# Turning the modulation's partial sums into columns: four products with a 0/1 matrix, or four transposes and a sum on VectorE

## The chip, the cores and the metric

One core of one Trainium2 chip runs the whole program in one launch. The metric is the device time of one execution in microseconds (us); a lower time is better. The engines are TensorE (PE, with its weight loads as PEld), VectorE (DVE), ScalarE (ACT), GpSimd (POOL) and SyncE (SP), which here only issues transfers.

## The reference, cut to what matters

Two blocks follow each other on a sequence of 256 tokens by 1024 channels, with a context of the same size. Both begin with a modulation: a condition vector and a context condition vector go through a large matrix, and the result, cut into pieces of 1024, scales, shifts and gates the tokens.

```
cond, cond_ctx = silu(c), silu(c_ctx)
mod   = cond     @ w_mod + b_mod      # 1024 -> 6*1024 (first block), 3*1024 twice (second)
mod_c = cond_ctx @ w_mod + b_mod
h  = rms_norm(x,   g) * (1 + sc1) + sh1
hc = rms_norm(ctx, g) * (1 + csc1) + csh1
y  = token_mixer(h, hc, ...)          # first block; then peer_ffn over 16384 experts
...                                   # second block: attention, pooling, neighbourhood attention
```

Everything is float32.

## The kernel before, in words

**The modulation.** The wide matrices are streamed in pieces of 128 x 1024. `mod_gen` computes 512 columns of one modulation: four pieces `mraw` arrive by SP's queue (L196), and eight matmuls per 512 columns (L211) write into one PSUM tile `modps`. The contraction of 1024 is cut into eight slices of 128; slice k goes to the row group 32*(k % 4), so that rows 32g and 32g+1 of `modps` hold the partial sum of group g for the two conditions, and the other rows are zero. VectorE copies `modps` to `modP` (L216). What is wanted is a column layout: channel on the partition, condition on the free axis. `mod_cols` makes it: for each of the four blocks of 128 columns a product with the 128 x 2 matrix `sel2`, which has ones at rows 32g+j of column j, adds the four groups and turns rows to columns at once (L231). VectorE adds the bias and writes the columns (L232). This runs 24 times: 4 times ahead of the first projection (`front`, tile `m`), 8 times beside the first block's mixers (`later`, tiles `m2`, `g1c`, `g2c`), 12 times beside the expert stage (`mods2`, tiles `mc` and `gc`).

**What runs around it.** Every large projection streams its weights: a piece `raw` arrives, ScalarE rounds it to `wH` (L78), VectorE subtracts to get `wL` (L79), and three matmuls (L116, L117, L118) use them. In the expert stage each of 128 tiles `ups` takes one such piece and 24 matmuls, while VectorE also does a top-k search. Then one-hot products (`pmps`, L992, `farps`, L977) pick activations, and 64 batches of four indirect loads `vrow` (L1035, issued by POOL) with eight matmuls `vacc` each (L1041) sum the chosen rows. The second half of these batches runs beside the second block's context half (`ch`, `ccat`). The rows fill 9 or 13 buffers, and a buffer comes free when its matmuls have run.

**What sets the order.** The engines execute in program order, each its own. The framework that builds the program sorts the instructions of each engine by times that it estimates itself; only those marked `keep_in_program_order` keep the written order. A change at 24 places therefore moves instructions elsewhere.

Of the kernel before, what the change touches and what calls it, by code (L numbers as in the profile page):

```python
# [15 lines left out]
ALU = mybir.AluOpType  # L16
AX = mybir.AxisListType
# [3 lines left out]
P = 128  # L21
# [23 lines left out]
class Builder:  # L45
# [178 lines left out]
    def mod_cols(self, dst, m, bias):  # L224


        nc = self.nc
        n = dst.shape[2]
        ps = self.ps((P, 4, 2), name="mcps")
        for b in range(4):  # L230
            nc.tensor.matmul(ps[:, b], m[:, b * P:(b + 1) * P], self.sel2, start=True, stop=True)  # L231
        nc.vector.tensor_tensor(dst, ps[:, :, 0:n], bias[:, :, None].to_broadcast([P, 4, n]), op=ALU.add)  # L232

    def row(self, dst, cols):

# [80 lines left out]
    def consts(self):  # L316
        cp, nc = self.cp, self.nc
        self.ident = self.load(cp, [P, P], "ident")
        self.sel2 = self.load(cp, [P, 2], "sel2")
        self.one = cp.tile([P, 1], F32, name="one")  # L320
        nc.gpsimd.memset(self.one, 1.0)
        self.bcol = self.load(cp, [P, 48], "b_cols")
        self.bcol2 = self.load(cp, [P, 2, 24], "b_cols_2")
        self.ms = cp.tile([P, 2, 2], F32, name="ms")
        self.half = cp.tile([P, 16], F32, name="half")
        nc.gpsimd.memset(self.half, -0.5)
        self.bp, self.Kc = None, []
        self.mcols = [cp.tile([P, 2, 8, 2], F32, name=f"mc{l}") for l in range(2)]
# [1240 lines left out]
def lay(i):  # L1569
    f = np.float32  # L1570
    r = {}
    tok = lambda a: np.ascontiguousarray(a.reshape(2, P, D).transpose(1, 0, 2))
    r["ident"] = np.eye(P, dtype=f)
    s2 = np.zeros((P, 2), f)
    for g in range(4):
        for j in range(2):
            s2[32 * g + j, j] = 1
    r["sel2"] = s2
    r["x"], r["ctx"] = tok(i["x"]), tok(i["ctx"])
    two = lambda a, b: np.ascontiguousarray(np.stack([a.reshape(D), b.reshape(D)], -1).reshape(8, P, 2).transpose(1, 0, 2))  # L1580
    r["cond"] = two(i["c"], i["c_ctx"])
# [7 lines left out]
    for d in range(2):  # L1589
        for typ in range(2):  # L1590
            dst = 32 * d + (64 if typ == 0 else 0)
# [90 lines left out]
```

## Time and profile before

| | |
|---|---|
| time, median of 3 runs | 1552.82 us (1551.61 to 1557.32) |
| the profiled execution | 1545.91 us, its span 1544.0 us |
| PE busy | 1436.1 us, 93% of the span |
| DVE busy | 924.0 us, 60% |
| ACT busy | 693.7 us, 45% |
| POOL busy | 383.1 us, 25% |
| mean granted clock of TensorE | 0.965 |

The span is the time from the first to the last instruction in the profiled execution; 1.9 us of its own time lie around it. A busy PE means that a matmul is in flight; matmuls overlap, so the distance between two starts tells more than the duration of one.

### The profile page before, as it was taken

To read this page: it belongs to the slowest core of one execution; us is meant where nothing else is said; L and a number is where in the kernel's file an instruction comes from. 1 tells how busy PE (TensorE), PEld (TensorE's weight loads), DVE (VectorE), ACT (ScalarE), POOL (GpSimd) and SP (SyncE) were. 2 spreads that over 40 slices of the span, in tenths; PEclk is the share of its full clock that TensorE was granted. 3 is DMA by queue.
4 is the path that set the end of the run, shared out by engine and by line. 5 is a ranking of instruction groups with operands and counts; after the bars stand their busy time and mean duration, and the time that the engine had idled before them with its cause. 6 is when DMAs were issued, how large, how long until landed. Compare 5 with 4: busy or idle time off the path is not lost.

```text
span 1544.0 us, 26118 instructions
## 1 busy us (share of the span) xinstructions
PE 1436.1 (93%) x10090; PEld 1122.3 (73%) x10090; DVE 924.0 (60%) x2284; ACT 693.7 (45%) x1152; POOL 383.1 (25%) x380
## 2 busy tenths in 40 slices
PE   7999997899999999999999998687979779998998
PEld 3677764798888899999977776334635458866976
DVE  4478464679998444444355554544334478867875
ACT  4354242444444455555444444332333355645653
POOL 1100001000000000000356664565567714012201
PEclk9999997999999999999989999798989999999999
DMA  9535344356886865666779997889998936414521
GB/s 358 167 132 171 108 133 150 125 172 213 306 290 241 304 187 186 190 189 186 238 306 349 357 353 289 305 308 341 344 334 280 349 121 209 153 55 155 182 80 41
DMA packets 97180, 345.80 MB, mean 224 GB/s; under 512 B 12705, under 2 KB 14241, under 8 KB 95777
## 3 DMA queue, kind: packets, MB, share of 16 engines
q1 hardware_dynamic: 54576, 198.73, 37.9%
q0 software_dynamic: 36864, 134.23, 23.7%
q10 hardware_dynamic: 5616, 11.18, 2.4%
q8 instruction: 79, 1.29, 0.3%
q14 instruction: 45, 0.36, 0.1%
HBM read 343.05 MB, written 1.05 MB: 223 GB/s over the span
## 4 chain that ended last, share of the span: by engine, by line
PE 86%; DMA 4%; DVE 4%; POOL 2%; issue 2%; ACT 2%; ACTq 0%; POOLq 0%; DVEq 0%
PE acc L116 10%; PE acc L118 10%; PE acc L117 9%; PE ups L116 8%; PE ups L118 8%; PE ups L117 8%; PE pmps L992 7%; PE vacc L1041 7%; PE modps L211 4%; DMA vrow<-in_v_dram,at 2%; PE tps L1491 2%; PE pvo L1497 2%; POOL vrow L1035 1%; PE mcps L231 1%; PE farps L977 1%
## 5 line engine op out<-in xcount | busy, mean ns | idle before, releaser
L79 DVE TENSOR_TENSOR wL<-raw,wH 128x1024 fp32r<-128x1024 f32 x269 | 337.1, 1253 | 245.9 <-ACT wH L78 244.5
L78 ACT CAST wH<-raw 128x1024 fp32r<-128x1024 f32 x277 | 290.3, 1050 | 369.2 <-PE ups L117 148.8
L1035 POOL DMA_INDIRECT vrow<-in_v_dram,at x256 | 252.8, 987 | 615.1 <-DVE wL L79 440.1
L116 PE MATMUL ups<-h2T,wH 128*128 128x256 f32 x1024 | 287.7, 281 | 0.0
L118 PE MATMUL ups<-h2T,wL 128*128 128x256 f32 x1024 | 286.5, 281 | 0.0
L117 PE MATMUL ups<-h2T,wH 128*128 128x256 f32 x1024 | 285.7, 279 | 0.0
L116 PEld LDWEIGHTS ups<-h2T,wH 128*128 128x128 f32 x1024 | 192.5, 188 | 14.3 <-issue 5.0
L118 PEld LDWEIGHTS ups<-h2T,wL 128*128 128x128 f32 x1024 | 192.1, 188 | 8.4 <-DVE tkc L826 1.7
L117 PEld LDWEIGHTS ups<-h2T,wH 128*128 128x128 f32 x1024 | 192.5, 188 | 0.0
L1041 PE MATMUL vacc<-vrow,Z 128*32 128x512 f32 x1024 | 147.4, 647 | 26.8 <-DMA vrow<-in_v_dram,at 26.8
L995 DVE SCALAR_TENSOR_TENSOR junk<-iota,sel,pmps 128x128 f32<-128x128 f32 x256 | 89.0, 348 | 96.2 <-PE pmps L992 89.5
L992 PE MATMUL pmps<-ATa,oh 128*128 128x72 f32 x512 | 104.8, 287 | 1.8 <-ACT oh L981 1.8
L992 PE MATMUL pmps<-ATb,oh 128*128 128x56 f32 x512 | 98.1, 274 | 0.0
L1041 PEld LDWEIGHTS vacc<-vrow,Z 128*32 128x32 f32 x1024 | 29.5, 114 | 89.6 <-issue 55.0
L980 ACT ACTIVATE oh<-farps,place 128x512 f32<-128x512 f32 x64 | 43.9, 687 | 87.0 <-PE farps L977 87.0
L992 PEld LDWEIGHTS pmps<-ATa,oh 128*128 128x128 f32 x512 | 80.2, 197 | 2.0 <-ACT oh L981 2.0
L992 PEld LDWEIGHTS pmps<-ATb,oh 128*128 128x128 f32 x512 | 80.3, 198 | 1.7 <-issue 1.7
L211 PE MATMUL modps<-mraw,condP 128*32 128x512 f32 x192 | 43.5, 677 | 16.5 <-DVE condP L186 8.3
L1480 ACT ACTIVATE smp<-sps,smst 128x512 f32<-128x512 f32 (+1 forms) x72 | 44.5, 619 | 28.9 <-DVE smst L1478 25.7
L921 ACT COPY ATa<-ups 128x256 f32<-128x256 f32 x72 | 47.5, 660 | 21.7 <-PE ups L118 21.7
L1478 DVE TENSOR_REDUCE smst<-sps 128x1 f32<-128x512 f32 (+1 forms) x72 | 42.5, 597 | 18.8 <-PE sps L1474 18.2
L116 PE MATMUL acc<-wL,xh 128*128 128x512 f32 (+1 forms) x128 | 48.4, 378 | 3.4 <-DVE wL L79 3.4
(407 smaller groups left out, 2926.2 us busy)
## 6 DMA issues: line engine op xcount, KB each, us to landing
raw<-in_u_dram SPq DMA_DIRECT2D x128, 512.0 KB, 3.8
mraw<-in_w_mod_dram SPq DMA_DIRECT2D x96, 512.0 KB, 4.5
raw<-in_w_in_dram SPq DMA_DIRECT2D x40, 512.0 KB, 4.9
raw<-in_w_out_dram SPq DMA_DIRECT2D x32, 512.0 KB, 3.6
raw<-in_w_gate_dram SPq DMA_DIRECT2D x24, 512.0 KB, 4.1
raw<-in_peer_wq_dram SPq DMA_DIRECT2D x16, 512.0 KB, 3.6
vrow<-in_v_dram,at POOLq DMA_INDIRECT x256, 6.3
raw<-in_w_nv_dram SPq DMA_DIRECT2D x8, 512.0 KB, 5.4
```

Of the source, the lines that this page charges most:

```text
L78: self.pin(nc.scalar.copy(H, raw))
L79: self.pin((low or nc.vector).tensor_sub(L, raw, H.bitcast(F32)))
L116: mm(ps, a[0], b[1], start=start, stop=False)
L117: mm(ps, a[0], b[0], start=False, stop=False)
L118: mm(ps, a[1], b[0], start=False, stop=stop)
L211: nc.tensor.matmul(ps[g:g + 32], cond[:, k], raw[k // 2][:, k % 2 * 512:(k % 2 + 1) * 512], start=k < 4, stop=k >= 4, tile_position=(0, g))
L921: nc.scalar.copy(acts[0][:, :, i1] if i1 < R0 else acts[1][:, :, i1 - R0], ps)
L992: nc.tensor.matmul(pm[:, i, r0:r1], oh[:, i], a[:, tb * P + t], start=True, stop=True)
L995: nc.vector.scalar_tensor_tensor(junk, self.iota, sel[:, 0, c:c + 1], pm[:, i], op0=ALU.is_equal, op1=ALU.mult, accum_out=act[:, c:c + 1])
L1035: nc.gpsimd.indirect_dma_start(v, None, rows, bass.IndirectOffsetOnAxis(ap=at[:, c:c + 1], axis=0))
L1041: tc.keep_in_program_order(nc.tensor.matmul(out[2 * tb + dh][32 * g:32 * g + 32], Z[:, b - b0, g], V[g][:, dh * 512:(dh + 1) * 512], start ...
L1480: nc.scalar.activation(p, ps, AF.Exp, bias=st[:, 0:1], accum_out=st[:, 1:2])
```

## The change

`mod_cols` transposes each 128 x 128 block of `modP` (by a matmul with the identity) into a PSUM tile of four times 128 columns. There the four partial sums of a condition lie 32 columns apart. VectorE sums over the four (a reduction that reads 4 x n x 4 elements per partition, n being 1 or 2, and writes 4 x n), and then adds the bias in place. The matrix `sel2` and its load fall away.

```
-        ps = self.ps((P, 4, 2), name="mcps")
+        ps = self.ps((P, 4, 4, 32), name="mcps")
         for b in range(4):
-            nc.tensor.matmul(ps[:, b], m[:, b * P:(b + 1) * P], self.sel2, start=True, stop=True)
-        nc.vector.tensor_tensor(dst, ps[:, :, 0:n], bias[:, :, None].to_broadcast([P, 4, n]), op=ALU.add)
+            nc.tensor.transpose(ps[:, b].rearrange("p g r -> p (g r)"), m[:, b * P:(b + 1) * P], self.ident)
+        nc.vector.reduce_sum(dst, ps[:, :, :, 0:n].rearrange("p b g r -> p b r g"), axis=AX.X)
+        nc.vector.tensor_tensor(dst, dst, bias[:, :, None].to_broadcast([P, 4, n]), op=ALU.add)
...
     def consts(self):
         cp, nc = self.cp, self.nc
         self.ident = self.load(cp, [P, P], "ident")
-        self.sel2 = self.load(cp, [P, 2], "sel2")
```

Lines behind `mod_cols` move by one up to `consts` (L288 becomes L289), and are the same behind it.

The order of the instructions changes at many places. Three matter here.

On PE, in the expert stage, the rows around one of the twelve calls (the 20th of 24), before:

```order
L116 MATMUL ups<-h2T_2390,wH 128x256
L117 MATMUL ups<-h2T_2388,wH 128x256
L231 MATMUL mcps<-sel_91,modP 128x2 x4
L118 MATMUL ups<-h2T_2388,wL 128x256
L116 MATMUL ups<-h2T_2391,wH 128x256
```

and of the change:

```order
L116 MATMUL ups<-h2T_2400,wH 128x256
L117 MATMUL ups<-h2T_2398,wH 128x256
L231 MATMUL mcps<-ident,modP 128x128 x4
L118 MATMUL ups<-h2T_2398,wL 128x256
L116 MATMUL ups<-h2T_2401,wH 128x256
```

Here nothing moved; four products have become four transposes at the same place.

On VectorE, at the end of `front`, where the second half of the channels gets its scale `a` and the affine step (`nhf`, `hT`) starts, before:

```order
L232 TENSOR_TENSOR m_75<-mcps,b_cols 128x8
L432 SCALAR_TENSOR_TENSOR a_77<-m_75,norm_g 128x8
L79 TENSOR_TENSOR wL<-raw,wH 128x1024
L288 TENSOR_SCALAR nhf<-xT,a_77,m_75 128x256 x3
L289 TENSOR_TENSOR hT_74<-nhf,hT_73 128x256 x2
```

and of the change:

```order
L79 TENSOR_TENSOR wL<-raw,wH 128x1024
L232 TENSOR_REDUCE m_75<-mcps 128x8
L233 TENSOR_TENSOR m_75<-m_75,b_cols 128x8
L432 SCALAR_TENSOR_TENSOR a_77<-m_75,norm_g 128x8
L289 TENSOR_SCALAR nhf<-xT,a_77,m_75 128x256 x3
L290 TENSOR_TENSOR hT_74<-nhf,hT_73 128x256 x2
```

The subtraction `wL` that stood between the scale and the affine step stands ahead of both now.

On PE, at the end of the expert rows, from the context's second norm (`nps<-ident,ctx`) on, with projections of the context left out at the dots, before:

```order
L1041 MATMUL vacc<-vrow,Z 32x512 x8
L278 MATMUL nps<-ident,ctx_9813 128x128 x16
L1041 MATMUL vacc<-vrow,Z 32x512 x8
...
L1041 MATMUL vacc<-vrow,Z 32x512 x2
...
L1041 MATMUL vacc<-vrow,Z 32x512 x14
L1321 MATMUL fps<-ident,kk 128x128 x12
```

and of the change:

```order
L1041 MATMUL vacc<-vrow,Z 32x512 x8
L279 MATMUL nps<-ident,ctx_9835 128x128 x16
L1041 MATMUL vacc<-vrow,Z 32x512 x8
...
L1041 MATMUL vacc<-vrow,Z 32x512 x8
...
L1041 MATMUL vacc<-vrow,Z 32x512 x10
L1321 MATMUL fps<-ident,kk 128x128 x2
L1041 MATMUL vacc<-vrow,Z 32x512 x6
L1321 MATMUL fps<-ident,kk 128x128 x6
L1041 MATMUL vacc<-vrow,Z 32x512 x8
```

Behind that norm stand 24 matmuls `vacc` (three batches) before, and 40 (five batches) now: two batches have moved behind it.

## Rows read from the trace of the kernel before

**Rows 1.** The page: busy time by engine, and the chain by engine

```profile
PE 1436.1 (93%) x10090; PEld 1122.3 (73%) x10090; DVE 924.0 (60%) x2284; ACT 693.7 (45%) x1152; POOL 383.1 (25%) x380
PE 86%; DMA 4%; DVE 4%; POOL 2%; issue 2%; ACT 2%; ACTq 0%; POOLq 0%; DVEq 0%
```

**Rows 2.** Windows: length, busy time of PE, PEld, DVE, ACT, POOL, clock, DMA

```profile
71.00:200.00 129.00, 129.00 (x777) 93.46 (x774) 83.68 (x154) 54.35 (x93) 5.10 (x5) 1.00 0.42 139
366.00:480.00 114.00, 114.00 (x899) 95.64 (x898) 109.68 (x388) 50.63 (x63) 0.00 (x0) 1.00 0.77 281
480.00:560.00 80.00, 80.00 (x662) 70.30 (x661) 44.91 (x56) 36.56 (x45) 0.00 (x0) 1.00 0.71 256
```

**Rows 3.** The view of the tile mcps: count, duration min/median/max in ns, first and last start

```profile
L231 PE MATMUL mcps<-sel,modP x192: 165/251/272, 16.9 to 552.1; 128*128 128x2 f32 x192
L232 DVE TENSOR_TENSOR mc<-mcps,b_cols x8: 141/156/166, 393.6 to 496.5; 128x8 f32<-128x8 f32 x8
```

**Rows 4.** Timeline of PE in the expert stage: start, length, instruction

```profile
429.70 0.95 PE L231 MATMUL mcps<-sel,modP 128*128 128x2 f32 x8
430.51 0.36 PE L116 MATMUL ups<-h2T,wH 128*128 128x256 f32 x1
```

**Rows 5.** Timeline of PE at four transposes in the mixers

```profile
133.18 0.60 PE L644 MATMUL kstp<-ident,de 128*128 128x128 f32 x4
133.53 0.37 PE L116 MATMUL acc<-hT,wH 128*128 128x256 f32 x1
```

**Rows 6.** Timeline of PE at the last two modulations of the mixers

```profile
256.46 1.05 PE L231 MATMUL mcps<-sel,modP 128*128 128x2 f32 x8 [1.22 <-DVE modP L216]
259.85 3.20 PE L211 MATMUL modps<-mraw,condP 128*32 128x512 f32 x8 [2.33 <-DMA mraw<-in_w_mod_dram]
269.97 1.05 PE L231 MATMUL mcps<-sel,modP 128*128 128x2 f32 x8 [0.80 <-DVE modP L216]
270.89 1.96 PE L241 MATMUL mrps<-modR,one 128*128 128x512 f32 x4
```

**Rows 7.** Timeline at the end of front, brackets: idle before and its releaser

```profile
45.29 0.95 PE L231 MATMUL mcps<-sel,modP 128*128 128x2 f32 x8
46.28 0.17 DVE L232 TENSOR_TENSOR m<-mcps,b_cols 128x8 f32<-128x8 f32 x1 [1.35 <-PE mcps L231]
46.56 1.22 DVE L79 TENSOR_TENSOR wL<-raw,wH 128x1024 fp32r<-128x1024 f32 x1
47.70 1.05 DVE L288 TENSOR_SCALAR nhf<-xT,a,m 128x256 f32<-128x256 f32 x3
49.14 0.39 PE L116 MATMUL acc<-hT,wH 128*128 128x256 f32 x1 [2.90 <-DVE hT L289]
```

**Rows 8.** Groups by line and shape, DVE: count, busy us, mean ns, idle before

```profile
L1478 DVE TENSOR_REDUCE smst<-sps 128x1 f32<-128x512 f32 x48 | 32.8, 687 | 7.2 <-PE sps L1474 6.8
L1478 DVE TENSOR_REDUCE smst<-sps 128x1 f32<-128x256 f32 x24 | 9.7, 417 | 11.6 <-PE sps L1474 11.4
L1268 DVE TENSOR_REDUCE hss<-raw 128x2 f32<-128x128 f32 x8 | 2.3, 284 | 3.4 <-ACT raw L1267 3.4
```

**Rows 9.** Timeline: a wL, and the first matmul that reads it

```profile
400.07 1.20 DVE L79 TENSOR_TENSOR wL<-raw,wH 128x1024 fp32r<-128x1024 f32 x1
403.07 0.28 PE L118 MATMUL ups<-h2T,wL 128*128 128x256 f32 x1
```

**Rows 10.** The view of line L644: the transposes of the tile kstp

```profile
L644 PE MATMUL kstp<-ident,de x16: 270/273/328, 97.9 to 145.3; 128*128 128x128 f32 x16
```

**Rows 11.** Waits of PE from 956 to 1244: us in total, times, longest

```profile
PE vacc L1041 <- DMA vrow<-in_v_dram,at: 26.8, 9, 5.7
```

**Rows 12.** Windows of the tile vacc: length, PE, PEld, DVE, clock, DMA share, GB/s

```profile
956.00:1244.00 288.00, 84.20 (x520) 16.04 (x520) 1.36 (x2) 0.91 0.88 319
```

**Rows 13.** Timeline: the first one-hot products, with the idle time before

```profile
764.88 0.44 PE L992 MATMUL pmps<-ATa,oh 128*128 128x72 f32 x2 [1.81 <-ACT oh L981]
```

**Rows 14.** Windows of all engines at the start of the one-hot products

```profile
767.00:781.00 14.00, 14.00 (x73) 10.89 (x71) 4.91 (x27) 5.45 (x8) 2.77 (x4) 0.51 0.56 226
```

More of the change, by code (lines that the diff above doesn't have):

```diff
@@ L1573, in lay @@
     r["ident"] = np.eye(P, dtype=f)
[L1574 to L1578, printed above, removed]
     r["x"], r["ctx"] = tok(i["x"]), tok(i["ctx"])
```

## The prediction

> **What bounds the kernel now.** I read the page first: PE is busy for 93% of the span, and the chain that ended last runs over PE for 86% of it [rows 1]. So time that PE saves should count, if it is saved where PE itself is the limit. Shares of a span don't tell that, so the windows by stage come next. From 71 to 200 us and from 366 to 560 us PE is busy for the whole window at a granted clock of 1.00 [rows 2]; the reader should look at DVE in the same rows: 109.68 of 114 us from 366 to 480, so there a second engine is nearly full. The view of the tile mcps says where the change sits: 192 matmul records for 24 calls, so eight records for four products, between 16.9 and 552.1 us [rows 3]. Of the 24 calls four lie ahead of 50 us, four from 71 to 200 us, four from 205 to 271 us, and twelve from 366 to 560 us.
>
> **What the products cost and what the transposes will.** A duration of 251 ns each [rows 3] is no price, because matmuls overlap. The price on PE is the distance from the first of a group to the next other instruction: 429.70 to 430.51, which is 0.81 us for eight records [rows 4]. Four transposes of 128 x 128 already stand in this kernel, each with one record: 133.18 to 133.53, which is 0.35 us [rows 5]. They write to PSUM and read float32 as the new ones do, so I take that price: a call saves 0.81 - 0.35 = 0.46 us of PE.
>
> - Expert stage, 12 calls: PE never pauses there, and the place of the call among its neighbours is unchanged (the first order extract). 12 x 0.46 = 5.5 us.
> - Mixers from 71 to 200 us, 4 calls, PE full too: 1.8 us.
> - 205 to 271 us, 4 calls. Behind the third PE waits 2.33 us for a transfer anyway [rows 6], so nothing is gained there. At the last, the row product follows in program order at 270.89, 0.92 us after the start at 269.97 [rows 6]; PE waits for modP ahead of it, so the saving shows at once. I count three calls at 0.4: 1.2 us.
> - Front, 4 calls. At the last one the reader can follow a latency: product at 45.29, columns at 46.28, a subtraction wL from 46.56, the affine step from 47.70, and PE, idle for 2.90 us, goes on at 49.14 [rows 7]. The transposes take 0.46 off that. The new order also puts wL ahead of the scale (the second extract), which would take up to 1.2 us more off, if the modulation's own pieces don't arrive later than that. The same swap stands at the first half of the channels. Bounds: 0 (transfers set the end) and 3 us (both swaps and the latency in full). I take 1.5 us, the middle, since PE works between these points and only part of what is moved away from the path comes back.
>
> Sum of what is saved: 5.5 + 1.8 + 1.2 + 1.5 = 10.0 us.
>
> **What is added.** A reduction on VectorE that reads 32 elements per partition (16 where n is 1) from PSUM, strided. The trace has no such size, but 512 elements took 687 ns, 256 took 417, and 128 (from SBUF) 284 [rows 8]; the slope is 270/256 = 1.05 ns per element, so 32 elements give 417 - 224 x 1.05 = 0.18 us. Bounds: 0.15 us, as short as an addition over 8 columns (156 ns [rows 3]), and 0.28 us, as the reduction over 128. I take 0.18. The addition of the bias stays, from SBUF; as long as now. So 24 x 0.18 = 4.3 us on VectorE. Where does it lie? In the expert stage behind the lead of wL: the wL that begins at 400.07 ends at 401.27, and the first matmul that reads it starts at 403.07, 1.80 us later [rows 9]. That is the shortest lead that I found from 366 to 480 us; the other tiles there have more. The seven calls there bring 7 x (0.46 + 0.18) = 4.5 us of drift against VectorE's 4.3 us of idle time in that window (114 - 109.68 [rows 2]), so the cover is just enough in the mean. If it weren't, PE would wait for wL. On the path the reduction stands only where PE waits for the columns, in front and at the last calls of the mixers: about six calls, 6 x 0.18 = 1.1 us. The load of sel2 (128 x 2) falls away; it lies beside the first pieces of x, and I count nothing: PE waits for those.
>
> Net: 10.0 - 1.1 = 8.9 us. Against the profiled execution 1545.91 - 8.9 = 1537.0 us. That execution was 6.9 us below the median of the runs (1552.82), so the same difference taken from the median gives 1552.82 - 8.9 = **1543.9 us**, 0.57% less. About 0.5% (7.8 us) is what a measurement of this kernel can tell from no change.
>
> [...] In the row, four transposes hold PE for 0.35 us, and PE's clock stays at 1.00 from 71 to 200 us with the 16 transposes of kstp inside it [rows 2, 5, 10]. [...]
>
> **The rivals.**
>
> *The new order helps further.* PE waits 26.8 us in nine waits for expert rows between 956 and 1244 us [rows 11]. With vacc moved behind context work (the third extract), each load has longer to land. If a quarter of that wait goes, 6.7 us more are saved: 1537 us. For it: VectorE and ACT aren't full there. Against: a later vacc frees its buffers later, and so the next load is issued later.
>
> *The new order gives the gain back.* From 956 to 1244 us 32 batches run, 9.0 us each, with the transfers 0.88 busy at 319 GB/s [rows 12]. A batch is four loads of 128 x 1024 float32, 2.1 MB, so 6.6 us at that rate. Two batches now stand behind the context's second norm that stood ahead of it. If one of them is exposed, 6.6 us come back: 1550.5 us. If the sum holds otherwise, this is "no change".
>
> *VectorE becomes the bound* from 366 to 480 us: the saving of seven calls there, 3.2 us, turns into waits for wL: 1547.1 us. For it is the full engine [rows 2], against it the lead [rows 9].
>
> *Slower.* The two batches are exposed at the full 9.0 us that one takes now, 18.0 us, because rows can only be issued when buffers come free: 1552.82 - 8.9 + 18.0 = 1561.9 us. It decides from 16.7 us on (8.9 + 7.8). Against it: the loads are ahead by up to nine buffers, more than two batches.
>
> [...]
>
> **How the numbers follow.** The sum holds, with the rest of the order worth at most 4 us either way: 0.45, 1540 to 1548 us, and a little more than half of that lies below 1545.1 us, the bound for "faster" (0.27 against 0.18). The order helps further: 0.20, all faster. The gain given back: 0.17, the same. VectorE the bound: 0.09, the same. Slower by exposed batches: 0.06; by the clock: 0.03. So faster 0.47, same 0.44, slower 0.09. The time is that of the likeliest case, rounded to 1544. The range goes down to 1536, which takes in the further help as priced and leaves about 0.07 of its case below, and up to 1555, past one exposed batch with VectorE as the bound on top (1553.7 us); above it remain the 0.09 of the slower cases. Both bounds of the reduction (0.15 and 0.28 us) move the net by 0.6 us at most, and both of the front by 1.5 us; they lie inside. The likeliest case alone has 1540 to 1548.
>
> **What would show it.** In the profile of the changed kernel: 96 records of mcps in place of 192; from a group's first transpose to the next matmul 0.35 to 0.42 us in the expert stage; the reduction at 0.15 to 0.28 us, 24 times; the distance from the first ups to the last shorter by some 5.5 us, with no wait of PE for wL in it; PE's restart at the end of front 1 to 2 us earlier. The prediction is wrong if that distance has not shrunk (then VectorE or the clock holds it), or if the stage from 956 us to the second block's first projection changes by more than 5 us in either direction; in that case the moved vacc decide and not the columns.

## The result: slower by 0.65%, and the profile after

The changed kernel takes 1564.45 us in the median of five runs (1561.95 to 1567.04), the kernel before 1553.62 us beside it (1551.61 to 1557.32). The ratio is 1.0065, with a 95% interval of 1.0037 to 1.0093: slower, by some 10 us, where 0.57% less was forecast. The median lies 9 us above the upper end of the forecast range, 1555 us.

The profiled execution of the changed kernel took 1567.04 us (span 1565.3), that of before 1545.91. So these two lie 21.1 us apart, twice as far as the medians: one is 2.6 us above its median, the other 7.7 below. A stage is taken as changed only where several kernels repeat it.

The page after, by engine, and the chain that ended last, answering to [rows 1]:

```profile
PE 1450.3 (93%) x9994; PEld 1119.6 (72%) x9994; DVE 929.9 (59%) x2308; ACT 692.9 (44%) x1152; POOL 387.5 (25%) x380
PE 82%; DMA 5%; DVE 5%; issue 3%; POOL 3%; ACT 2%; ACTq 0%; POOLq 0%; SPq 0%; DVEq 0%
```

PE has 96 records fewer and is busy 14.2 us longer. That alone tells that neither a wait nor a transfer is the first thing to look for: work on PE has become longer somewhere. The windows answer to [rows 2] (length, then busy time of PE, PEld, DVE, ACT, POOL, granted clock, DMA share, GB/s):

```profile
71.00:200.00 129.00, 129.00 (x761) 90.49 (x760) 82.07 (x156) 52.23 (x87) 5.09 (x5) 1.00 0.42 136
366.00:480.00 114.00, 114.00 (x879) 93.87 (x878) 107.83 (x394) 50.11 (x63) 0.00 (x0) 1.00 0.80 289
480.00:560.00 80.00, 80.00 (x649) 68.66 (x648) 50.55 (x70) 36.14 (x46) 0.00 (x0) 1.00 0.72 253
```

The clock is still at 1.00 with the transposes inside, and VectorE is no fuller from 366 to 480 us, where it was nearly full. The view of the tile mcps, answering to [rows 3] and [rows 8]:

```profile
L231 PE MATMUL mcps<-ident,modP x96: 270/273/477, 16.4 to 553.6; 128*128 128x128 f32 x96
L232 DVE TENSOR_REDUCE m<-mcps x8: 164/180/191, 19.2 to 170.2; 128x8 f32<-128x32 f32 x4, 128x4 f32<-128x16 f32 x4
L232 DVE TENSOR_REDUCE mc<-mcps x8: 160/187/191, 396.0 to 498.8; 128x8 f32<-128x32 f32 x8
```

The parts of the change cost what the sum said: the reduction 0.16 to 0.19 us, and on PE's timeline, answering to [rows 4], a group to the next matmul 478.13 - 477.78 = 0.35 us:

```profile
477.78 0.60 PE L231 MATMUL mcps<-ident,modP 128*128 128x128 f32 x4
478.13 0.36 PE L116 MATMUL ups<-h2T,wH 128*128 128x256 f32 x1
...
866.88 1.05 PE L1041 MATMUL vacc<-vrow,Z 128*32 128x512 f32 x2
867.86 0.40 PE L977 MATMUL farps<-far,identb 128*128 128x128 bf16 x4
868.19 1.92 PE L1041 MATMUL vacc<-vrow,Z 128*32 128x512 f32 x14
870.03 0.44 PE L992 MATMUL pmps<-ATa,oh 128*128 128x72 f32 x2
```

The last four rows are the loss. In the stage of the one-hot products a batch of `vacc` (eight products, 16 records) is in two pieces here, with the four matmuls `farps` between them: the first product alone holds PE for 0.98 us (866.88 to 867.86), the other seven for 1.84 us (868.19 to 870.03). Before, the eight ran in one piece. Timeline of PE before, in the same stage:

```profile
852.90 1.92 PE L1041 MATMUL vacc<-vrow,Z 128*32 128x512 f32 x16
854.76 0.40 PE L977 MATMUL farps<-far,identb 128*128 128x128 bf16 x4
```

1.86 us. Each product writes one group of 32 columns (`tile_position=(0, 32 * g)`, in the order 3, 2, 1, 0, twice), and products of different groups run side by side: 16 records of about 0.59 us lie in 1.92 us. Counted up to the start of the next matmul, a product alone takes 0.98 us and four take 0.99 or 1.00 (d_mid below), seven take 1.84 and eight 1.86. So this cut costs 0.98 + 1.84 - 1.86 = 0.96 us (0.97 in the mean of the twelve cuts counted below), and PE counts as busy through it. Windows of the tile vacc alone from 805 to 960 us, first before, then after (length, PE, PEld, DVE, clock, DMA share, GB/s):

```profile
805.00:960.00 155.00, 50.02 (x416) 10.85 (x416) 0.00 (x0) 1.00 0.93 338
```

```profile
805.00:960.00 155.00, 57.59 (x384) 11.40 (x384) 0.00 (x0) 1.00 0.93 330
```

26 batches in 50.02 us are 1.92 each, 24 in 57.59 are 2.40: fewer batches in more time, at the same clock. The order of PE's instructions in the changed kernel shows the place as written in the program:

```
L992 MATMUL pmps<-ATb,oh 128x56
L1041 MATMUL vacc<-vrow,Z 32x512
L977 LDWEIGHTS identb
L977 MATMUL farps<-far,identb 128x128
L1041 MATMUL vacc<-vrow,Z 32x512 x7
L977 LDWEIGHTS identb
```

Twelve of the 31 batches of this stage are cut so, six into 1 and 7, six into 2 and 6; before, none is. Counted in turns of four products side by side, the 248 products take 62 turns before and 74 after. The stage runs from the first farps to the last pmps. Of the changed kernel, the views of the two tiles:

```profile
L977 PE MATMUL farps<-far,identb x256: 219/219/315, 763.8 to 973.6; 128*128 128x128 bf16 x128
L992 PE MATMUL pmps<-ATb,oh x512: 262/275/421, 766.5 to 979.1; 128*128 128x56 f32 x171
```

and before:

```profile
L977 PE MATMUL farps<-far,identb x256: 219/219/314, 762.4 to 956.4; 128*128 128x128 bf16 x128
L992 PE MATMUL pmps<-ATb,oh x512: 262/275/462, 765.2 to 959.9; 128*128 128x56 f32 x171
```

215.27 us against 197.44: 17.8 us. From the 21st of the 64 groups of pmps on, where all the cuts lie, it is 142.16 against 128.76 us, 13.4 us. Counted from each start to the next, 11.6 of them are in vacc (50.6 against 39.0 us), as twelve cuts at 0.97 give, 1.7 in farps (11.3 against 9.6), some of which are broken up as well, and 0.1 in pmps. Ahead of that group lie 4.4 us more; the granted clock from 762 to 805 us is 0.76 there and 0.84 before, but this piece differs by up to 7.5 us among the first eight kernels below, so these 4.4 us aren't put down to the cuts.

### The profile page after: what moved, and what is told of

The parts are those of the page before. It is cut to its first block, busy times and chain, and to the rows that moved or that the text cites. A ratio compares the mean times of both kernels' runs of the same rounds, so it can differ in the third digit from the quotient of the medians.

```text
span 1565.3 us, 25949 instructions
## 1 busy us (share of the span) xinstructions
PE 1450.3 (93%) x9994; PEld 1119.6 (72%) x9994; DVE 929.9 (59%) x2308; ACT 692.9 (44%) x1152; POOL 387.5 (25%) x380
## 4 chain that ended last, share of the span: by engine, by line
PE 82%; DMA 5%; DVE 5%; issue 3%; POOL 3%; ACT 2%; ACTq 0%; POOLq 0%; SPq 0%; DVEq 0%
PE acc L116 9%; PE acc L118 8%; PE acc L117 8%; PE ups L116 8%; PE ups L118 8%; PE ups L117 8%; PE vacc L1041 8%; PE pmps L992 7%; PE modps L211 4%; DMA vrow<-in_v_dram,at 2%; PE tps L1491 2%; POOL vrow L1035 2%; PE pvo L1497 2%; DMA mraw<-in_w_mod_dram 1%; PE farps L977 1%
## 5 line engine op out<-in xcount | busy, mean ns | idle before, releaser
L79 DVE TENSOR_TENSOR wL<-raw,wH 128x1024 fp32r<-128x1024 f32 x269 | 331.5, 1233 | 238.6 <-ACT wH L78 237.1
L1041 PE MATMUL vacc<-vrow,Z 128*32 128x512 f32 x1024 | 157.2, 640 | 19.8 <-DMA vrow<-in_v_dram,at 19.8
```

What stands on the lines that cost most here:

```text
L79: self.pin((low or nc.vector).tensor_sub(L, raw, H.bitcast(F32)))
L1041: tc.keep_in_program_order(nc.tensor.matmul(out[2 * tb + dh][32 * g:32 * g + 32], Z[:, b - b0, g], V[g][:, dh * 512:(dh + 1) * 512], start ...
```

## The experiments

The **cuts** theory: the new order cuts groups of products that run side by side, and that costs more than the columns win. Its rival, the **columns** theory: the transposes and reductions themselves cost more than the products, by their time or by the clock. A third, **moved batches**: the two batches that now stand behind the context's second norm. "The stage" is the one above. The first four kernels ran on one chip, beside the kernel before at 1552.0 us, the next four on a second, beside 1553.5 us; the last four ran on a third, on which the kernel before takes 1585.9 us, so of those the ratio counts.

**The change, with its batches held together (a_hold).** The first product of a batch waits for all four rows, so that nothing is ready to be sorted between the eight:

```
+ for ld in loads[:3] if (dh, g) == (0, 3) else ():
+     tc.add_manual_dep(mm.ins, ld.ins.name, mybir.DependencyInfo(
+         mybir.DependencyClass.Sync, mybir.DependencyReason.DATA))
```

> The changed kernel, with one edge added: the first of the eight products vacc of a batch waits for all four expert rows, so nothing can be sorted between the eight. Cuts theory (the new order cuts twelve batches of vacc between 764 and 980 us, and a cut costs about 0.97 us because products in different groups of 32 columns no longer run side by side): the stage from the first farps to the last pmps shrinks by 11.6 us, from 215.2 to about 203.6 us; behind it nine more cuts go, of which some lie behind the rows' transfers, 0 to 8 us. Time 1564.5 - 11.6 = 1552.8 us, down to 1545. Columns theory (transposes and reductions cost more than the products): no change, 1564 us. Moved-batches theory (two batches stand later): no change in the stage, 1564 us within 3.

Measured: 1543.43 us (12 runs), ratio to before 0.9951 (0.9933 to 0.9969). The transposes are all there, and the kernel is faster than before. Views of farps and pmps:

```profile
L977 PE MATMUL farps<-far,identb x256: 219/219/314, 764.1 to 960.1; 128*128 128x128 bf16 x128
L992 PE MATMUL pmps<-ATb,oh x512: 262/275/420, 766.8 to 965.6; 128*128 128x56 f32 x171
```

The stage is 201.6 us, 13.7 less than in the changed kernel (11.6 expected), and behind it, to the last vacc, 278.6 us are left of 287.9: 9.3 us, with nine cuts gone. The columns theory, which wanted no change, falls. The moved batches aren't tested by this kernel alone, for the new sorting put one of the two ahead of the norm again (32 matmuls vacc stand behind it).

**The kernel before, with its batches held together (b_hold).** The same edge.

> The kernel before with the same edge. The stage of the one-hot products has no cut in either, so it stays at 197.4 us within 1; behind it twelve cuts of vacc go. Cuts theory: 0 to 11 us less there, since part of that stage waits for rows: 1543 to 1553.6 us. Columns and moved-batches theories: no change, 1553.6 us.

Measured: 1562.16 us, ratio 1.0076 (1.0052 to 1.0100): slower, a miss. The stage is 199.1 us, as expected. Behind it twelve cuts went, and to the last vacc it took 291.0 us and not 285.6. PE waits there for more: 12.3 us for `ctx` and 10.9 for `kk` and its piece, against 10.5 and 5.7 before. The edge re-sorts that part of the program too, and it may be that fewer turns don't show where PE waits for VectorE and for rows anyway. The profiled execution is 16.4 us longer than that of before and loses in every part (3.3 us ahead of ups, 1.6 in it, 1.6 in the stage, 5.4 behind it, 4.4 after the last vacc), so why the kernel lost 10 us stays open.

**The kernel before, with twelve batches in another order of groups (b_cut12).**

```
+ quads = [(dh, g) for dh in range(2) for g in (3, 2, 1, 0)]
+ if b in range(8, 20):
+     quads.insert(1, quads.pop(4))
```

> The kernel before, in which twelve batches of vacc (8 to 19) issue two products of the same row group behind each other, so that eight products need three turns of four and not two; nothing else in the order moves. Cuts theory: the price of a lost turn is 0.93 to 0.97 us also without any foreign instruction in between, so the stage grows by 11.2 to 11.6 us to about 209 us, and the time to 1553.6 + 11.4 = 1565 us. If the price of a cut is one of switching to another instruction and not of the lost turn: no change, 1553.6 us. Columns and moved-batches theories: no change.

Measured: 1552.4 us, ratio 1.0016 (0.9995 to 1.0036), and the stage 197.5 us: no price at all, a miss. The 16 records still take 1.86 us (855.61 to 857.47):

```profile
855.61 1.93 PE L1043 MATMUL vacc<-vrow,Z 128*32 128x512 f32 x16
857.47 0.40 PE L977 MATMUL farps<-far,identb 128*128 128x128 bf16 x4
```

In the trace the second record of each of these twelve batches starts 13 to 14 ns behind the first, in the batches around them 6 to 7 ns, and the batch as a whole is no longer for it. So two products of the same column group right behind each other cost nothing here, and my picture of strict turns was wrong. What a piece takes at a granted clock of 1.00 goes by the number of products in its fullest column group: with one there it is 0.98 to 0.99 us (the pieces of one and of two products in the changed kernel), with two 1.84 to 1.86 us (the pieces of six, seven and eight). The matmul behind a piece uses the whole array, and it starts 0.07 us before the end of the piece's last record (by the profile, which models these ends), behind every piece of this stage before and in the changed kernel. So the first piece takes its 0.98 us, and the rest still takes 1.84: that is what a cut costs.

**The kernel before, with modps issued from the last piece to the first (b_modrev).** Products with the 0/1 matrix, no transposes; the sorting then cuts the same twelve batches.

```
- for k in range(2 * j - 2, 2 * j + 2) if j % 2 else ():
+ for k in range(2 * j + 1, 2 * j - 3, -1) if j % 2 else ():
```

> The kernel before, with its products with the 0/1 matrix, in which the four products modps of a pair of pieces are issued from the last piece to the first; the sorted order that comes of it cuts twelve batches of vacc in the stage of the one-hot products, as the change's does, and six cuts fewer of modps in the expert stage. Cuts theory: that stage grows by 11.6 us to about 209 us, the expert stage shrinks by 6 x 0.93 = 5.6 us, the mixers by 0.9; time 1553.6 + 11.6 - 6.5 = 1558.7 us, down to 1555 if front gains too. Columns theory: no transposes, so no loss: 1553.6 us or less, and the stage of the one-hot products stays at 197.4 us.

Measured: 1556.72 us, ratio 1.0018 (0.9995 to 1.0042).

```profile
L977 PE MATMUL farps<-far,identb x256: 219/219/314, 765.0 to 973.8; 128*128 128x128 bf16 x128
L992 PE MATMUL pmps<-ATb,oh x512: 262/275/420, 767.7 to 979.3; 128*128 128x56 f32 x171
```

The stage takes 214.3 us without a single transpose, and 142.16 us from the 21st group on, as in the changed kernel to the hundredth; the pieces of vacc, farps and pmps follow each other in the same order there. The time as a whole can't be told from that of before, since the interval holds 1, and the profiled execution, at 1563.68 us, was the slowest of the twelve; it is the stage that answers the question. The expert stage won 2.2 us, where 5.6 were expected: 3.9 in its first half, where the calls stand, less 1.6 in the second, where none stands and where b_hold and p_early lose the same.

**Transposes in the twelve early calls alone (p_early), and in the twelve of the expert stage alone (p_exp).** The other calls keep product and addition (the condition is `> 12` for the second):

```
+ self.ncols = getattr(self, "ncols", 0) + 1
+ if not (self.ncols <= 12):
+     ps = self.ps((P, 4, 2), name="mcps")
...
```

> Transposes and reductions in the twelve calls of front and of the mixers alone; the twelve calls of the expert stage keep the products. The sorted order has no cut of vacc between the first and the last pmps (31 groups of eight), and modps is cut once more among the mixers. Cuts theory: the stage of the one-hot products stays at 197.4 us within 1; the mixers win 4 x 0.45 us and lose 0.93: time 1552 - 1 to 3 = 1549 to 1551 us, no difference that can be told. Columns theory (transposes or reductions cost in front or let the clock fall there): slower by 5 us or more, with the loss ahead of 275 us.

> Transposes and reductions in the twelve calls of the expert stage alone. The sorted order has the twelve cuts of vacc that the changed kernel has, and three turns of modps more than before in the expert stage. Cuts theory: expert stage 12 x 0.40 - 3 x 0.93 = 2 us shorter, stage of the one-hot products 214 us as in the changed kernel (197.4 before), time 1552 + 15 = 1564 to 1567 us. Columns theory: what the early calls cost is gone, so less than the changed kernel's loss: about 1555 us.

Measured: 1553.26 us, ratio 0.9978 (0.9958 to 0.9999), and 1564.6 us, ratio 1.0070 (1.0041 to 1.0100). The late twelve alone bring the whole loss, 11.3 us between these two medians. Their last pmps, p_early and then p_exp (the stage began at 767.5 and 761.0 us):

```profile
L1000 PE MATMUL pmps<-ATb,oh x512: 262/275/420, 770.2 to 966.5; 128*128 128x56 f32 x171
```

```profile
L1000 PE MATMUL pmps<-ATb,oh x512: 262/275/422, 763.8 to 976.4; 128*128 128x56 f32 x171
```

199.1 and 215.3 us. So no transpose stands inside the stage that loses; all of them lie at least 200 us ahead of it, and act on it through the order alone. p_exp speaks against the moved batches too: it has one of them behind the norm, and its stretch from the last pmps to the last vacc, 284.6 us, is no longer than before (285.6).

**One edge for modps, in the changed kernel (a_h2) and in the one before (b_h2).** The first of four products modps waits for both pieces; vacc is left alone, and the sorting happens to leave its batches whole in both.

```
+ if k % 4 == 0:
+     self.tc.add_manual_dep(mm.ins, self.mld.ins.name, mybir.DependencyInfo(
+         mybir.DependencyClass.Sync, mybir.DependencyReason.DATA))
```

> The changed kernel, with one edge added in the modulation: the first of four products modps waits for both of their pieces. vacc is left to the sorting, which then makes no cut in the stage of the one-hot products. Cuts theory: that stage at 197 to 199 us; modps in the expert stage runs in 26 turns of four, not 34: 8 x 0.93 = 7.4 us less there than in the changed kernel, so ups from first to last about 397 us (404.9 in the changed kernel, 406.4 before); time 1564.4 - 16 - 7.4 = 1541 us. Columns theory: no faster than before, 1552 us or more, since all 24 calls still transpose.

> The kernel before with the same edge for modps: 25 turns in the expert stage and not 31, so 5.6 us less there, ups about 401 us, and no cut in the stage of the one-hot products (197.4 us); time 1552 - 6 = 1546 us by the cuts theory. Against the changed kernel with the edge it shows what the columns are worth where the orders agree: 12 x 0.40 - 0.93 = 3.9 us in the expert stage, about 1 in the mixers, so 4 to 6 us in all for the transposes. By the columns theory the products win by some 5 us.

Measured: 1545.23 us, ratio 0.9946 (0.9925 to 0.9968), and 1549.54 us, ratio 0.9975 (0.9954 to 0.9996). From the first to the last matmul `ups` takes 398.5 us with transposes, 401.4 with products (406.4 before), 2.9 us for the columns, where 3.9 were expected. The view of the tile ups, a_h2 and then b_h2:

```profile
L116 PE MATMUL ups<-h2T,wH x1024: 277/280/388, 352.5 to 750.7; 128*128 128x256 f32 x171
L118 PE MATMUL ups<-h2T,wL x1024: 274/280/390, 352.8 to 751.0; 128*128 128x256 f32 x171
```

```profile
L116 PE MATMUL ups<-h2T,wH x1024: 277/280/390, 358.8 to 760.0; 128*128 128x256 f32 x171
L118 PE MATMUL ups<-h2T,wL x1024: 274/280/390, 359.1 to 760.2; 128*128 128x256 f32 x171
```

Part of what stands against more is seen in the windows of a_h2:

```profile
366.00:480.00 114.00, 113.32 (x922) 96.21 (x920) 111.19 (x386) 53.04 (x67) 0.00 (x0) 1.00 0.79 291
```

and in PE's waits from 359 to 766 us:

```profile
PE ups L118 <- DVE wL L79: 0.7, 1, 0.7
```

PE waits for wL here, and VectorE is busy for 111.19 of 114 us. In the changed kernel wL led by 1.16 us or more; in a_h2 the shortest lead is 0.05. With the cuts of modps gone, VectorE has little left to give here, though one wait of 0.7 us is all that it has cost so far.

**Twelve extra products, behind the first product of a batch (d_in), or behind the fourth (d_mid).** The kernel before; the extra product works into a tile that nobody reads. In d_mid the place is `(1, 3)`.

```
+ if b in range(8, 20) and (dh, g) == (0, 2):
+     tc.keep_in_program_order(nc.tensor.matmul(self.ps((P, 8), name="xtra"),
+         self.ident, self.ident[:, 0:8], start=True, stop=True))
```

> The kernel before with twelve extra products (the identity with 8 of its columns, into a tile that nobody reads), each put behind the first of the eight products of a batch of vacc (batches 8 to 19), so that they run as 1 and 7. By the runs that the traces show (1: 0.98 us, 7: 1.85 us, 8 in one piece: 1.86 us) a batch costs 0.97 us more: the stage of the one-hot products grows by 11.6 us and by what the twelve products take themselves (0.1 to 0.2 us each), to 210 to 212 us; time 1553 + 13 = 1566 us. If it were the extra instructions and not their place: as with the extra products in the middle.

> The same twelve extra products, each behind the fourth of the eight, so that a batch runs as 4 and 4: two full turns as in one piece. Cuts theory: only the products themselves and the switch, 0.1 to 0.3 us each, so the stage grows by 1 to 4 us to about 200 us, 8 to 11 us less than with the extra products behind the first; time 1554 to 1557 us. If any break of a batch costs the same: as with the extra products behind the first, 1566 us.

Measured: ratios 1.0026 (1.0002 to 1.0050) and 0.9989 (0.9961 to 1.0018): of the 13 us expected of d_in some 4 show, d_mid can't be told from before. Timeline of PE, d_in:

```profile
846.75 1.05 PE L1044 MATMUL vacc<-vrow,Z 128*32 128x512 f32 x2
847.73 0.39 PE L1042 MATMUL xtra<-ident 128*128 128x8 f32 x2
848.04 1.92 PE L1044 MATMUL vacc<-vrow,Z 128*32 128x512 f32 x14
849.89 0.40 PE L977 MATMUL farps<-far,identb 128*128 128x128 bf16 x4
```

and d_mid:

```profile
840.56 1.06 PE L1044 MATMUL vacc<-vrow,Z 128*32 128x512 f32 x8
841.55 0.39 PE L1042 MATMUL xtra<-ident 128*128 128x8 f32 x2
841.87 1.06 PE L1044 MATMUL vacc<-vrow,Z 128*32 128x512 f32 x8
842.87 0.40 PE L977 MATMUL farps<-far,identb 128*128 128x128 bf16 x4
```

The same instructions take 3.14 us and 2.31 us; twelve times the difference is 10.0 us. This is the clean price: a break at 4 and 4 costs 0.13 us (0.99 + 1.00 - 1.86), a break at 1 and 7 costs 0.97. In the whole stage 7.2 us show (235.5 against 228.2 us), in the time 0.37%, some 6 us. On that chip the stage runs some 30 us longer in all four kernels, at a granted clock of 0.92 from 764 to 980 us in d_in and with 7.5 us of waits of PE for `oh`, so a part of a cut may lie beside waits there; that isn't shown.

**The changed kernel with both edges (a_hold2), and with every reduction done twice (a_hold_red2).** The second has the edge for vacc and a second `reduce_sum` into the same place.

> The changed kernel with both edges: vacc waits for its four rows, modps for its two pieces. No cut in the stage of the one-hot products, 26 turns of modps in the expert stage, no cut of vacc behind it (nine to twelve there otherwise). Cuts theory: as the changed kernel with the edge for modps alone (1545 us) or less, since the cuts behind 960 us go too, of which a part lies behind the rows' transfers: 1537 to 1545 us. Columns theory: 1552 us or more.

> The changed kernel with the edge for vacc, and each of the 24 reductions done twice into the same place, so VectorE works some 0.2 us longer per call, 5 us in all. If the reduction lies beside other work but for the calls of front: within 2 us of the same kernel with one reduction (1543.4 us), and ups from first to last 404 to 405 us. If VectorE is the bound in the expert stage: up to 2.5 us longer there and up to 5 us in all, 1548 us.

Measured: ratios 0.9899 (0.9865 to 0.9933) and 0.9975 (0.9950 to 1.0000). Both edges together have the lowest ratio of all, 1.0% below the kernel before and about what was expected; whether they beat one edge alone isn't shown, since a_hold (0.9933 to 0.9969) and a_h2 ran on other chips and the intervals meet. The doubled reductions leave `ups` at 404.3 us (404.9 with single ones), so VectorE's time in them is covered there. The ratio is 0.24 points above that of a_hold, 3.7 us where 2 at most were expected, but the two come from different chips, with different orders and with intervals that overlap, so it can't tell whether the reductions cost anything elsewhere.

## Why the prediction was wrong

**The step that failed** is the one on the order: "The sum holds, with the rest of the order worth at most 4 us either way", with the batches behind the context's second norm as the only place where more was priced. I read the order for instructions that had moved past others and asked what waits for them. What decided is which instructions stand next to each other: twelve batches cut in the stage of the one-hot products, 13.4 us from the 21st group on, while the order of that stage was in no term and no rival; [rows 13] and [rows 14] show its start alone. The first sign of being wrong that the prediction named, that `ups` from first to last doesn't shrink, did not appear (406.4 to 404.9 us), and so it didn't point there. The signs of the cuts were there: batches in pieces stand in the third order extract, and a batch of 16 records of 0.59 us in 1.92 us stands on the timeline before.

Point by point:

- *Transposes, 0.35 us and not 0.81.* Right where a matmul of ups follows, as in the one call that the first order extract shows. Behind six of the twelve calls (five before) stands modps, and there a group takes 0.53 us (0.88 before). Twelve calls won 4.8 us (10.07 us before, 5.29 after, from each group to the next matmul), forecast 5.5; the mixers' four 1.7, forecast 1.8.
- *Expert stage 5.5 us shorter.* It was 1.6 us shorter in the profile. The columns won 4.8, and modps gave 2.8 back: 34 turns of four and not 31, three cuts at 0.93 us, the same mechanism; 0.4 us are left over. Among the mixers one more cut took 1.0 of the 1.7 us.
- *205 to 271 us, 1.2 us.* Nothing of it came. From each group to the next matmul the three calls that were counted took 1.38, 1.37 and 0.91 us before, and 1.34, 1.39 and 0.91 after. In the first two PE now waits longer for what VectorE makes of the columns, as here at the first, before and then after:

```profile
213.34 0.91 PE L750 MATMUL mlsps<-qT,kT 128*128 128x256 f32 x3 [0.42 <-DVE g1c L232]
```

```profile
216.81 0.92 PE L750 MATMUL mlsps<-qT,kT 128*128 128x256 f32 x3 [0.74 <-DVE g1c L232]
```

- *Reduction 0.18 us, covered by the lead of wL.* Right: 0.16 to 0.19 us, and no wait for wL in the changed kernel. "VectorE becomes the bound" was not this kernel's trouble; a_h2 comes near it (VectorE busy for 111.19 of 114 us, one wait for wL of 0.7 us).
- *Front 1.5 us, bounds 0 and 3.* Wrong in sign here: the first `alps`, the product behind the first projection, starts at 74.4 us, not 71.3 (70.8 to 71.4 in before, b_hold, b_cut12 and p_exp, which share the order of front, and 74.3 in a_hold, so this is no scatter). The end of it did get shorter, as read (45.29 to 49.14 before, 3.85 us; 48.02 to 51.16 after, 3.14 us), but its last modps come later:

```profile
47.95 1.22 DVE L79 TENSOR_TENSOR wL<-raw,wH 128x1024 fp32r<-128x1024 f32 x1
48.02 0.66 PE L231 MATMUL mcps<-ident,modP 128*128 128x128 f32 x4 [0.79 <-DVE modP L216]
49.09 0.18 DVE L232 TENSOR_REDUCE m<-mcps 128x8 f32<-128x32 f32 x1
49.71 1.06 DVE L289 TENSOR_SCALAR nhf<-xT,a,m 128x256 f32<-128x256 f32 x3
51.16 0.58 PE L116 MATMUL acc<-hT,wH 128*128 128x256 f32 x1 [2.48 <-DVE hT L290]
```

  The reduction starts only when the wL that moved ahead of it is nearly done (47.95 to 49.17 us), so the shorter group gains nothing there (1.07 us from its first transpose to the reduction, 0.99 from the first product to the addition before); what got shorter is the way from the columns to the affine step, 0.62 us and not 1.42. With modps held together the first `alps` starts at 67.4 us with transposes (a_h2) and at 67.7 with products (b_h2): the columns are worth next to nothing there, and the order of modps 3.6 us (b_h2 against before).
- *The order helps further* and *gives the gain back*, both priced in the rows from 956 us on. PE's waits for rows fell, answering to [rows 11]:

```profile
PE vacc L1041 <- DMA vrow<-in_v_dram,at: 16.8, 7, 5.0
```

  and over the whole execution they are 19.8 us, 26.8 before; but the stretch from the last pmps to the last vacc took 287.9 us and not 285.6. The two moved batches decided nothing.
- *Slower by the clock*, a chance of 0.03: no run shows a clock that falls behind transposes. The granted clock is 1.00 from 71 to 200 and from 366 to 560 us with the transposes inside; from 200 to 275 us it is 0.91, and was 0.89; from 0 to 71 us it is 0.93, was 0.95, and is 0.90 in b_modrev, which has no transposes for the columns. A transpose is 273 ns long in the median, but that is a duration and no price: four of them hold PE for 0.35 us ahead of a matmul of ups, 0.53 us ahead of modps.

The columns' own worth, orders being near alike, is a_h2 against b_h2: 1545.23 against 1549.54 us on one chip, about 0.3%. So the mechanism forecast is there at about half its size (4.3 us of 8.9, and 2.9 of 5.5 in the expert stage), and the order it came with cost more. The 2.9 us are the firmer of the two: in these two profiles 4.7 us of the difference lie at the start of the stage (65.7 against 70.3 us ahead of the 21st group), where neither a call nor a cut stands. Of the 10.8 us between the medians of the change and of before the stage of the one-hot products explains all and more. The 3 us lost in front don't reach ups for certain: its first matmul starts between 355.9 and 359.2 us in those four kernels, at 358.8 in the changed one. How much of what follows 980 us is scatter of single executions, two profiles can't tell. The 29 runs of the kernel before beside a_hold alone reach from 1541.0 to 1558.0 us.

## What to carry to other kernels

When a framework sorts the instructions, compare the new order not only for what has moved but for groups that lost their neighbours: count the pieces into which every group that shares PE's array is cut, and price a cut by the busiest column group of each piece (here 0.98 us with one product in it, 1.84 to 1.86 with two). A local edit 200 us away can change them. Where such groups matter, tie the first instruction to the last of the group's inputs, so that all are ready together; that took some 20 us off the changed kernel, but in the kernel before the same edge lost 10, so it is measured and not assumed.

## What the runs showed of the hardware that was not expected

Two products of the same group of 32 columns right behind each other did not hold back those of other groups: eight in the order 3, 3, 2, 1, 0, 2, 1, 0 take the same 1.86 us as in the order 3, 2, 1, 0, 3, 2, 1, 0 (b_cut12). One alone takes 0.98 us up to the next matmul, four take 0.99 and 1.00 (d_mid). From 805 to 960 us PE shows as busy for all 155 us at a granted clock of 1.00 before, in b_cut12, and in the changed kernel with its pieces of one product, so a busy share of 100% doesn't tell whether one product runs or four.
